# Feed-forward blocks with tokens as the stationary operand and the norm factor in the activation

## The chip, the cores and the metric

The kernel runs on one core of a Trainium2 chip. TensorE (PE) multiplies matrices and transposes, ScalarE (ACT), VectorE (DVE) and GpSimd (POOL) do the work on elements, SyncE (SP) issues the transfers. The metric is the time of one execution on the device in microseconds (us), as the median of several runs.

## The reference

Two stacks of layers over 256 tokens of 1024 channels, all in float32. Around each mixer (recurrent, attention, gated delta rule, short convolution, sparse attention; six in all) stand two feed-forward blocks, twelve in all, and they are what the change is about:

```
def swiglu_2(h, w_gate_up, w_down):              # F = 2816 hidden columns
    g, u = jnp.split(h @ w_gate_up, 2, axis=-1)
    return (jax.nn.silu(g) * u) @ w_down

f = swiglu(rms_norm(h, ffn1_pre_g[layer]), ffn1_w_gate[layer], ffn1_w_up[layer], ffn1_w_down[layer])
h = h + 0.5 * rms_norm(f, ffn1_post_g[layer])    # first stack, 4 blocks: a gain after the block ("post")
h = h + 0.5 * swiglu_2(rmsnorm(h, ffn_norm[layer, 0]), ...)   # second stack, 8 blocks: none
```

`rms_norm(x, g)` is `x * rsqrt(mean(x * x) + eps) * g`. The `shared_kv` of the first stack projects another norm of the same input that a block gets.

## The kernel before

Every product of float32 operands is made of three matmuls, on operands split into a high and a low part (`mm3`, L162 to L164). Weights come through `weights` (L125 to L157): SP loads a unit of 1024 columns into one of five `raw` buffers, ACT writes its high part (L154 with the gain of the norm as a scale, L150 without), DVE the low part (L155, L151). The high and low parts of the gate and up weights live in a pool of six buffers, those of the down weights in another of six.

The 256 tokens are two tiles of 128 (`t` = 0 and 1). `h[t]` is the residual stream in SBUF. `prep` (L194) makes the operand of the next projection: squares on ACT (`rstd`, L189), a small sum on DVE (L190), the power on POOL (L191), then `xn`, the normalized tile, on DVE (L208; L210 where the gain is multiplied in as a row, which holds for the norms before the mixers). Eight transposes of `xn` on PE (L174), a copy on ACT (L175, `xh`) and a subtraction on DVE (L176, `xl`) follow in `flush`.

A block (`ffn`) walks over the hidden columns in 11 groups of 256. Group 0 goes by `rows_group`: tokens are stationary, the weights move 512 columns wide (256 of gate, 256 of up), 24 matmuls for each token tile, and the result has to be transposed. Groups 1 to 10 go by `cols_group`: weights are stationary in pieces of 128 x 128, both token tiles move (256 columns), 96 matmuls for a group; the result is already transposed. `act` (L244 on ACT, L245 and L246 on DVE) makes `hid`, and L292 and L293 split it into `hh` and `hl`. `down_mm` multiplies with the down weights, 12 matmuls of 512 columns for each token tile and group, and runs one group behind. At the end of a block `residual` adds to `h[t]`: L340 without a gain after the block; with one, the squares of the accumulators (L189), a product (L335) and a sum (L336). It then calls `prep`.

The order of the instructions on each engine is fixed when the program is built, by a scheduler that takes the order of the code, the buffers that come free and a priority; the weight conversions are raised by `ahead` places. PSUM has four banks for the accumulators (`acc`), two for the gate and up products (`gu`) and two for transposes (`tr`).

Of the kernel before, what the change touches and what calls it, by code (L numbers as in the profile page):

```python
# [64 lines left out]
class Core:  # L65
# [44 lines left out]
    def rows_to_cols(self, name, *srcs):  # L110
        """srcs: DRAM [n, w] each -> SBUF [w, sum n] with row r in column r."""
# [47 lines left out]
    def mm3(self, out, l, r, start, stop, skip=False):  # L159
        """out += l.T @ r for operands split in (high, low) parts."""  # L160
# [5 lines left out]
    def split_T(self, src, xh, xl):  # L166
        """transpose the 128-column chunks of src [128, *] into xh/xl [128, chunks, 128]"""
# [10 lines left out]
    def by_token(self):  # L178
        """a pair [128, 2, 8, 128] (token tile, chunk, token), high and low"""
# [3 lines left out]
    def rstd(self, parts, scale=1.0):  # L183
        """(mean square of two 512 column parts + eps) ** -0.5, times scale"""
# [6 lines left out]
        nc.gpsimd.tensor_tensor(ss[:, 3:4], ss[:, 2:3], self.mhalf[:, :1], op=OP.pow)  # L191
        return ss[:, 3:4]

    def prep(self, t):  # L194
        """transposed split of h[t], normalized (times row_gain, where there is one), into self.x; the
        transposes are left to flush"""
        nc = self.nc
        self.flush()
        if t == 0:
            self.x = self.by_token()  # L200
        h = self.h[t]
        r = self.rstd([h[:, 0:512], h[:, 512:1024]])
        x, xs = self.x, []
        for n in range(2):
            xn = self.work.tile([128, 512], F32, name="xn", bufs=2)
            s = slice(n * 512, n * 512 + 512)
            if self.row_gain is None:
                nc.vector.tensor_scalar_mul(xn, h[:, s], r)  # L208
            else:
                nc.vector.scalar_tensor_tensor(xn, h[:, s], r, self.row_gain[:, s], op0=OP.mult, op1=OP.mult)  # L210
            xs.append(xn)
# [1211 lines left out]
```

## Time and profile before

| | |
|---|---|
| median of 3 runs | 3331.24 us (3331.01 to 3331.54) |
| the profiled execution: span | 3325.6 us |
| the profiled execution's own time | the span and what lies around it; against the median this is 5.6 us |
| PE, DVE, ACT, POOL busy | 98%, 65%, 54%, 2% |
| chain that ended last | PE 88%, DVE 6%, ACT 3% |
| bytes moved | 543.94 MB, mean 164 GB/s |

A page of the profile describes one execution; its rows name an engine, a line of the kernel, the operands (`out<-in`), and times. Busy time of an engine that nobody waits for costs nothing; what counts is when PE starts its instructions, since PE has work nearly all the time. PEld is the load of the stationary operand, which overlaps with PE.

### The profile page before, as it was taken

The page shows a single profiled execution, that of the slowest core. Times are in us where ns is not written, and L with a number is a line of the kernel's source. Part 1 is how long each engine was busy: PE and PEld are TensorE (multiplying, and loading weights), DVE is VectorE, ACT ScalarE, POOL GpSimd, SP SyncE. Part 2 cuts the span into 40 slices and gives each one's busy share as a digit, 9 for nine tenths or more (in the row PEclk, how much of TensorE's full clock was granted, in tenths as well). Part 3 has the DMA queues.
Part 4 walks back from the last instruction along what each step waited for, and adds up shares of the span by engine and source line. Part 5 has one row for each costly group of instructions (what it writes and reads, how often), then busy time and mean ns, then how long its engine had stood idle before and what let it go on. Part 6 is the DMA issues. An engine that isn't in the chain of part 4 may idle for free.

```text
span 3325.6 us, 57379 instructions
## 1 busy us (share of the span) xinstructions
PE 3266.9 (98%) x22022; PEld 2950.3 (89%) x22022; DVE 2163.9 (65%) x4039; ACT 1781.7 (54%) x3277; POOL 82.1 (2%) x106
## 2 busy tenths in 40 slices
PE   8999999999999999999999999999999999999999
PEld 8988898988798998989999989899767989989898
DVE  7667766664666657776566575665767566577764
ACT  6557655554555544555555455554566555454653
POOL 0000000000000000000000000000100000000000
PEclk9999999998899999999999999999999999999999
DMA  8643665644465663336656466566515656532463
GB/s 265 193 132 120 216 198 169 186 152 129 145 192 160 208 185 109 102 99 206 189 178 198 145 198 195 158 206 188 143 52 164 186 161 205 179 102 86 133 201 109
DMA packets 422043, 543.94 MB, mean 164 GB/s; under 512 B 36232, under 2 KB 369096, under 8 KB 421768
## 3 DMA queue, kind: packets, MB, share of 16 engines
q1 hardware_dynamic: 421768, 540.27, 52.6%
q8 instruction: 173, 2.83, 0.3%
q14 instruction: 102, 0.84, 0.1%
HBM read 539.12 MB, written 1.05 MB: 162 GB/s over the span
## 4 chain that ended last, share of the span: by engine, by line
PE 88%; DVE 6%; ACT 3%; issue 2%; POOL 1%; DMA 1%; POOLq 0%; SPq 0%; ACTq 0%; DVEq 0%
PE ps L164 26%; PE ps L162 26%; PE ps L163 26%; PE ps L174 1%; PE ps L892 1%; PE ps L898 1%; DVE wlo L155 1%; PE ps L1286 1%; DVE wlo L151 1%; POOL ss L191 1%; PE ps L1310 1%; PE ps L725 1%; ACT sq L189 1%; PE ps L554 1%; ACT whi L150 0%
## 5 line engine op out<-in xcount | busy, mean ns | idle before, releaser
L162 PE MATMUL ps<-xh,whi 128*128 128x256 f32 (+1 forms) x4704 | 1335.0, 284 | 6.7 <-ACT v L839 2.7
L164 PE MATMUL ps<-xh,wlo 128*128 128x256 f32 (+1 forms) x4704 | 1333.7, 284 | 0.0
L163 PE MATMUL ps<-xl,whi 128*128 128x256 f32 (+1 forms) x4704 | 1332.8, 283 | 0.0
L155 DVE SCALAR_TENSOR_TENSOR wlo<-raw,gains,whi 128x512 fp32r<-128x512 f32 (+1 forms) x1024 | 717.1, 735 | 470.8 <-ACT whi L154 457.3
L154 ACT ACTIVATE whi<-raw,gains 128x512 fp32r<-128x512 f32 (+1 forms) x1024 | 676.7, 707 | 560.1 <-issue 265.3
L162 PEld LDWEIGHTS ps<-xh,whi 128*128 128x128 f32 (+1 forms) x4704 | 895.6, 190 | 14.1 <-ACT v L839 3.1
L163 PEld LDWEIGHTS ps<-xl,whi 128*128 128x128 f32 (+1 forms) x4704 | 895.9, 190 | 6.0
L164 PEld LDWEIGHTS ps<-xh,wlo 128*128 128x128 f32 (+1 forms) x4704 | 895.3, 190 | 1.2
L151 DVE TENSOR_TENSOR wlo<-raw,whi 128x1024 fp32r<-128x1024 f32 (+4 forms) x473 | 569.6, 1209 | 270.4 <-ACT whi L150 268.0
L150 ACT CAST whi<-raw 128x1024 fp32r<-128x1024 f32 (+4 forms) x473 | 488.9, 1038 | 298.9 <-DMA raw<-in_ffn_w_down 126.0
L162 PE MATMUL ps<-whi,hh 128*128 128x512 f32 x1056 | 412.7, 391 | 0.0
L163 PE MATMUL ps<-wlo,hh 128*128 128x512 f32 x1056 | 412.6, 391 | 0.0
L164 PE MATMUL ps<-whi,hl 128*128 128x512 f32 x1056 | 411.3, 390 | 0.0
L162 PE MATMUL ps<-whi,xh 128*128 128x512 f32 (+3 forms) x624 | 249.2, 400 | 3.0 <-ACT xh L175 3.0
L164 PE MATMUL ps<-whi,xl 128*128 128x512 f32 (+3 forms) x624 | 245.4, 394 | 2.4 <-DVE xl L176 2.4
L163 PE MATMUL ps<-wlo,xh 128*128 128x512 f32 (+3 forms) x624 | 246.0, 394 | 0.0
L164 PEld LDWEIGHTS ps<-whi,hl 128*128 128x128 f32 x1056 | 197.8, 188 | 43.3 <-DVE hl L293 1.8
L162 PEld LDWEIGHTS ps<-whi,hh 128*128 128x128 f32 x1056 | 198.8, 188 | 38.8 <-ACT hh L292 2.0
L163 PEld LDWEIGHTS ps<-wlo,hh 128*128 128x128 f32 x1056 | 198.3, 188 | 37.5
L244 ACT ACTIVATE hid<-ps 128x256 f32<-128x256 f32 x264 | 99.7, 378 | 132.5 <-PE ps L164 132.2
L245 DVE SCALAR_TENSOR_TENSOR hid<-hid,ps 128x256 f32<-128x256 f32 x264 | 110.2, 418 | 74.4 <-ACT hid L244 74.3
L164 PEld LDWEIGHTS ps<-whi,xl 128*128 128x128 f32 (+2 forms) x624 | 116.7, 187 | 28.1 <-DVE xl L176 6.8
(403 smaller groups left out, 2757.2 us busy)
## 6 DMA issues: line engine op xcount, KB each, us to landing
raw<-in_ffn_w_gate_up SPq DMA_DIRECT2D x704, 256.0 KB
raw<-in_ffn_w_down SPq DMA_DIRECT2D x264, 512.0 KB
raw<-in_ffn_w_gate SPq DMA_DIRECT2D x176, 256.0 KB
raw<-in_ffn_w_up SPq DMA_DIRECT2D x176, 256.0 KB
raw<-in_gdn_w_in SPq DMA_DIRECT2D x64, 512.0 KB
raw<-in_sc_w_in SPq DMA_DIRECT2D x24, 512.0 KB
raw<-in_w_kv SPq DMA_DIRECT2D x16, 512.0 KB
raw<-in_gdn_w_out SPq DMA_DIRECT2D x16, 512.0 KB
```

Source lines behind the costliest of these rows:

```text
L150: nc.scalar.copy(hi, raw)
L151: nc.vector.tensor_sub(lo, raw, f32(hi))
L154: nc.scalar.activation(hi[:, i], raw[:, i], AF.Copy, scale=gain[i])
L155: nc.vector.scalar_tensor_tensor(lo[:, i], raw[:, i], gain[i], f32(hi[:, i]), op0=OP.mult, op1=OP.subtract)
L162: mm(out, l[0], r[0], start=start, stop=False, skip_group_check=skip)
L163: mm(out, l[0], r[1], start=False, stop=False, skip_group_check=skip)
L164: mm(out, l[1], r[0], start=False, stop=stop, skip_group_check=skip)
L174: nc.tensor.transpose(p[:, k], src[:, (i + k) * 128:(i + k + 1) * 128], self.ident)
L189: nc.scalar.activation(sq, p, AF.Square, scale=1 / (32.0 * scale), accum_out=ss[:, i:i + 1])
L191: nc.gpsimd.tensor_tensor(ss[:, 3:4], ss[:, 2:3], self.mhalf[:, :1], op=OP.pow)
L244: nc.scalar.activation(hid, p[:, :256], AF.Tanh, scale=0.5)
L245: nc.vector.scalar_tensor_tensor(hid, hid, 1.0, p[:, :256], op0=OP.add, op1=OP.mult)
```

## The change

All groups now run with the tokens stationary. `G(j, t)` is the gate and up product of group `j` and tile `t`, 24 matmuls of 512 columns; `T(j)` transposes the four pieces of `hid`; `D(j, t)` is the down product, 12 matmuls. `prep` no longer normalizes where there is no row gain: `h` itself is transposed, and half of the norm factor goes into a tile `half[t]`, computed after the transposes are issued. `act` takes it: the tanh gets it as scale, and the second product 2 times its square. `shared_kv`, which projects the same operand, multiplies the factor in afterwards.

The order of the code: at the start of a block tile 0 goes two groups ahead before tile 1 is transposed, and at the end tile 0 is finished, and its norm started, before tile 1 has its last gate product. Down weights of a group are shared out over two pools (`wts`, and `fw` with six more buffers).

```diff
-        r = self.rstd([h[:, 0:512], h[:, 512:1024]])
...
+        if self.row_gain is None:
+            self.half[t] = self.work.tile([128, 2], F32, name="half", bufs=6)
+            xs = halves
+        else:
+            r, xs = self.rstd(halves), []
...
         if t == 1:
             self.flush()
+        if self.row_gain is None:
+            f = self.half[t]
+            self.rstd(halves, 0.5, f[:, 0:1])
+            nc.vector.tensor_scalar(f[:, 1:2], f[:, 0:1], f[:, 0:1], 2.0, op0=OP.mult, op1=OP.mult)
...
+        hp = ctx.enter_context(self.tc.tile_pool(name="hid", bufs=2))
+        own = ctx.enter_context(self.tc.tile_pool(name="fw", bufs=6))
...
+            gu[j] = [self.weights([(0, gv[:, 2 * kk:2 * kk + 2, c]), (256, uv[:, 2 * kk:2 * kk + 2, c])],
+                                  [gain[:, 2 * kk + i:2 * kk + i + 1] for i in range(2)],
+                                  pool=self.wts if kk < 2 or j == 0 else own) for kk in range(4)]
...
+            dw[j] = [self.weights([(0, dv[:, 2 * j + k:2 * j + k + 1, :])], None, (1, 1024),
+                                  self.wts if k == 0 and j < 9 else own) for k in range(2)]
...
+        def G(j, t):
+
+            p = self.bank("gu")
+            for k in range(8):
+                wh, wl = gu[j][k // 2]
+                self.mm3(p, (xh[:, t, k], xl[:, t, k]), (wh[:, k % 2], wl[:, k % 2]), k == 0, k == 7)
...
+            nc.scalar.activation(h, p[:, :256], AF.Tanh, scale=half[t][:, 0:1])
+            nc.vector.scalar_tensor_tensor(h, h, 1.0, p[:, :256], op0=OP.add, op1=OP.mult)
+            nc.vector.scalar_tensor_tensor(h, p[:, 256:], half[t][:, 1:2], h, op0=OP.mult, op1=OP.mult)
...
+        def T(j, ts=(0, 1)):
...
+            self.split_T(hid[j][:, 128 * c.start:128 * c.stop], *[a[:, c] for a in hT[j]])
...
+        load_gu(0)
+        G(0, 0)
+        load_gu(1)
+        G(1, 0)
+        self.flush()
+        G(0, 1)
+        G(1, 1)
+        T(0)
+        load_d(0)
+        D(0, 0)
+        T(1)
+        D(0, 1)
+        for j in range(2, 10):
+            load_gu(j)
+            G(j, 0)
+            load_d(j - 1)
+            G(j, 1)
+            D(j - 1, 0)
+            T(j)
+            D(j - 1, 1)
...
+        load_gu(10)
+        G(10, 0)
+        load_d(9)
+        D(9, 0)
+        load_d(10)
+        T(10, (0,))
+        D(10, 0)
+        self.residual(0, acc[0], pg, 0.5)
+        G(10, 1)
+        D(9, 1)
+        self.flush()
+        T(10, (1,))
+        D(10, 1)
+        self.residual(1, acc[1], pg, 0.5)
```

How the instructions stand now is shown at three places. First PE in the middle of a block, where the gate product ends and the down product begins; before (`xh`, `xl` tokens, `whi`, `wlo` weights, `hh`, `hl` hidden values):

```order
L162 MATMUL ps<-xh,whi 128x256
L163 MATMUL ps<-xl,whi 128x256
L164 MATMUL ps<-xh,wlo 128x256
L162 MATMUL ps<-whi,hh 128x512
L163 MATMUL ps<-wlo,hh 128x512
L164 MATMUL ps<-whi,hl 128x512
```

Now, where the second half of the down product of the group before begins:

```order
L162 MATMUL ps<-whi,hh 128x512
L163 MATMUL ps<-wlo,hh 128x512
L164 MATMUL ps<-whi,hl 128x512
L174 MATMUL ps<-ident,hid 128x128 x4
L162 MATMUL ps<-whi,hh 128x512
L163 MATMUL ps<-wlo,hh 128x512
L164 MATMUL ps<-whi,hl 128x512
L162 MATMUL ps<-whi,hh 128x512
```

Four transposes of `hid` stand between the two halves of the down product, twelve matmuls behind the last gate matmul.

Second, DVE over one group in the middle of a block, before (L155 and L151 are weight conversions, L245 and L246 the two products of `act`, L293 the split):

```order
L155 SCALAR_TENSOR_TENSOR wlo<-raw,gains,whi 128x512 x6
L245 SCALAR_TENSOR_TENSOR hid<-hid,ps 128x256
L246 SCALAR_TENSOR_TENSOR hid<-hid,ps 128x256
L155 SCALAR_TENSOR_TENSOR wlo<-raw,gains,whi 128x512
L293 TENSOR_TENSOR hl<-hid,hh 128x256
L245 SCALAR_TENSOR_TENSOR hid<-hid,ps 128x256
L155 SCALAR_TENSOR_TENSOR wlo<-raw,gains,whi 128x512
L246 SCALAR_TENSOR_TENSOR hid<-hid,ps 128x256
L293 TENSOR_TENSOR hl<-hid,hh 128x256
L151 TENSOR_TENSOR wlo<-raw,whi 128x1024 x2
```

Now (L271 and L272 are the two products, L176 the split behind the transposes):

```order
L271 SCALAR_TENSOR_TENSOR hid<-hid,ps 128x256
L272 SCALAR_TENSOR_TENSOR hid<-ps,half,hid 128x256
L155 SCALAR_TENSOR_TENSOR wlo<-raw,gains,whi 128x512 x6
L271 SCALAR_TENSOR_TENSOR hid<-hid,ps 128x256
L155 SCALAR_TENSOR_TENSOR wlo<-raw,gains,whi 128x512
L272 SCALAR_TENSOR_TENSOR hid<-ps,half,hid 128x256
L155 SCALAR_TENSOR_TENSOR wlo<-raw,gains,whi 128x512
L176 TENSOR_TENSOR hl<-ps,hh 128x512
```

The second tile's products still have one weight conversion between them, and the split of both tiles is one instruction.

Third, PE at the end of a block that another block follows, where tile 0 is transposed; before:

```order
L164 MATMUL ps<-whi,hl 128x512
L174 MATMUL ps<-ident,xn 128x128 x8
L162 MATMUL ps<-whi,hh 128x512
L163 MATMUL ps<-wlo,hh 128x512
L164 MATMUL ps<-whi,hl 128x512
```

Now:

```order
L164 MATMUL ps<-whi,hl 128x512
L174 MATMUL ps<-ident,h_90 128x128 x8
L162 MATMUL ps<-whi,xh 128x512
L163 MATMUL ps<-wlo,xh 128x512
L162 MATMUL ps<-whi,xh 128x512
L163 MATMUL ps<-wlo,xh 128x512
L174 MATMUL ps<-ident,hid 128x128 x2
L164 MATMUL ps<-whi,xl 128x512
L162 MATMUL ps<-whi,xh 128x512
L163 MATMUL ps<-wlo,xh 128x512
```

`h_90` is `h[0]`. Before, down matmuls of tile 1 followed the transposes; now the gate matmuls of the next block that read their result do, and tile 1's transposes of `hid` stand among them.

## Rows read from the trace of the kernel before

**Rows 1.** The page: the first section (busy time, share of the span and instructions of each engine) and the fourth (the chain that ended last, by engine and by line).

```profile
PE 3266.9 (98%) x22022; PEld 2950.3 (89%) x22022; DVE 2163.9 (65%) x4039; ACT 1781.7 (54%) x3277; POOL 82.1 (2%) x106
...
PE 88%; DVE 6%; ACT 3%; issue 2%; POOL 1%; DMA 1%; POOLq 0%; SPq 0%; ACTq 0%; DVEq 0%
PE ps L164 26%; PE ps L162 26%; PE ps L163 26%; PE ps L174 1%; PE ps L892 1%; PE ps L898 1%; DVE wlo L155 1%; PE ps L1286 1%; DVE wlo L151 1%; POOL ss L191 1%; PE ps L1310 1%; PE ps L725 1%; ACT sq L189 1%; PE ps L554 1%; ACT whi L150 0%
```

**Rows 2.** The view of instructions grouped by line, engine and operands, different shapes apart: busy us, mean ns of one, and after the second bar the idle time of the engine just before them with what ended it. PE's duration of a matmul overlaps the next one's, so the pace is read from starts (Rows 3).

```profile
L162 PE MATMUL ps<-xh,whi 128*128 128x256 f32 x4512 | 1280.8, 284 | 4.7 <-ACT v L839 2.7 <-ACT whi L150 2.0
...
L155 DVE SCALAR_TENSOR_TENSOR wlo<-raw,gains,whi 128x512 fp32r<-128x512 f32 x984 | 702.0, 747 | 465.6 <-ACT whi L154 452.1 <-DMA raw<-in_ffn_w_gate_up 8.9 <-DMA raw<-in_ffn_w_up 1.5
L154 ACT ACTIVATE whi<-raw,gains 128x512 fp32r<-128x512 f32 x984 | 661.5, 717 | 557.0 <-issue 265.3 <-PE ps L163 219.8 <-DMA raw<-in_ffn_w_gate_up 42.7
...
L162 PE MATMUL ps<-whi,hh 128*128 128x512 f32 x1056 | 412.7, 391 | 0.0
...
L162 PE MATMUL ps<-whi,xh 128*128 128x512 f32 x544 | 220.8, 406 | 2.8 <-ACT xh L175 2.8
...
L164 PE MATMUL ps<-whi,xl 128*128 128x512 f32 x544 | 217.3, 400 | 2.4 <-DVE xl L176 2.4
...
L174 PE MATMUL ps<-ident,xn 128*128 128x128 f32 x288 | 42.2, 284 | 24.2 <-DVE xn L208 15.2 <-DVE xn L210 8.1 <-DVE future L92 0.4
```

**Rows 3.** Windows over one group in the middle of a block: from the start of its first gate matmul (1000.07) to the start of its first down matmul (1011.58) to the start of the next group (1017.05), and the two together. Columns: length, busy time and instructions of each engine, granted TensorE clock as a share of full speed, share of the DMA engines, GB/s.

```profile
1000.07:1011.58 11.51, 11.51 (x98) 11.51 (x96) 5.04 (x8) 4.39 (x7) 0.00 (x0) 1.00 0.58 184
1011.58:1017.05 5.47, 5.47 (x27) 4.51 (x25) 4.93 (x10) 4.21 (x7) 0.00 (x0) 1.00 0.62 193
1000.07:1017.05 16.98, 16.98 (x122) 16.02 (x120) 9.96 (x17) 8.60 (x14) 0.00 (x0) 1.00 0.60 187
```

**Rows 4.** The timeline of PE in a mixer that projects with tokens stationary: matmuls of 512 columns on `xh`, and between two of them four transposes. Columns: start, duration, engine, line, operation, operands.

```profile
1870.20 0.39 PE L162 MATMUL ps<-whi,xh 128*128 128x512 f32 x1
...
1870.88 0.39 PE L162 MATMUL ps<-whi,xh 128*128 128x512 f32 x1
1871.11 0.60 PE L439 MATMUL ps<-ident,y 128*128 128x128 f32 x4
1871.47 0.47 PE L163 MATMUL ps<-wlo,xh 128*128 128x512 f32 x1
1871.78 0.39 PE L164 MATMUL ps<-whi,xl 128*128 128x512 f32 x1
1872.01 0.40 PE L162 MATMUL ps<-whi,xh 128*128 128x512 f32 x1
```

**Rows 5.** The timeline at the end of the gate matmuls of group 0, tile 0, of the first block (the part that already has tokens stationary): the last gate matmul, the activation on ACT, the two products on DVE with a weight conversion between them, and the transposes of `hid`.

```profile
20.66 0.39 PE L164 MATMUL ps<-whi,xl 128*128 128x512 f32 x1
...
21.09 0.39 ACT L244 ACTIVATE hid<-ps 128x256 f32<-128x256 f32 x1 [1.65 <-PE ps L164]
...
21.51 0.42 DVE L245 SCALAR_TENSOR_TENSOR hid<-hid,ps 128x256 f32<-128x256 f32 x1 [0.28 <-ACT hid L244]
...
21.85 0.74 DVE L155 SCALAR_TENSOR_TENSOR wlo<-raw,gain,whi 128x512 fp32r<-128x512 f32 x1
...
22.51 0.41 DVE L246 SCALAR_TENSOR_TENSOR hid<-hid,ps 128x256 f32<-128x256 f32 x1
...
23.16 0.38 PE L174 MATMUL ps<-ident,hid 128*128 128x128 f32 x2
```

**Rows 6.** The timeline at the end of a block without a gain after it (the norm before the next block): `h` is written, PE runs its last down matmul before the wait, the normalized `xn` is made, PE transposes it.

```profile
1666.46 0.69 DVE L340 SCALAR_TENSOR_TENSOR h<-ps,h 128x512 f32<-128x512 f32 x1 [0.23 <-PE ps L164]
...
1668.75 0.39 PE L164 MATMUL ps<-whi,hl 128*128 128x512 f32 x1
1668.82 0.88 DVE L208 TENSOR_SCALAR xn<-h,ss 128x512 f32<-128x512 f32 x2 [0.66 <-POOL ss L191]
...
1669.36 1.11 PE L174 MATMUL ps<-ident,xn 128*128 128x128 f32 x8 [0.22 <-DVE xn L208]
```

**Rows 7.** The same at blocks with a gain after them: squares of the accumulators on ACT (L189), the sum into `h` on DVE (L336) and the transposes; the first two of a block before the recurrent mixer, tile 0 (there the norm that follows has a row gain), the last four of a block before another block, tile 0 and tile 1.

```profile
196.04 0.60 ACT L189 ACTIVATE sq<-ps 128x512 bf16<-128x512 f32 x1
...
202.79 1.32 PE L174 MATMUL ps<-ident,xn 128*128 128x128 f32 x8 [1.35 <-DVE xn L210]
...
523.07 0.60 ACT L189 ACTIVATE sq<-ps 128x512 bf16<-128x512 f32 x1 [0.24 <-PE ps L164]
...
526.05 1.28 DVE L336 TENSOR_TENSOR h<-xn,h 128x512 f32<-128x512 f32 x2
...
528.66 0.58 ACT L189 ACTIVATE sq<-ps 128x512 bf16<-128x512 f32 x1
...
535.15 0.69 DVE L336 TENSOR_TENSOR h<-xn,h 128x512 f32<-128x512 f32 x1
```

**Rows 8.** The timeline of the same block end, tile 1: the eight transposes and the next matmul that reads them.

```profile
538.46 1.06 PE L174 MATMUL ps<-ident,xn 128*128 128x128 f32 x8 [0.86 <-DVE xn L208]
...
539.76 0.50 PE L162 MATMUL ps<-whi,xh 128*128 128x512 f32 x1 [0.24 <-ACT xh L175]
```

**Rows 9.** Windows, columns as in Rows 3: the longest stretch at half the clock, in the attention, and the same length after it.

```profile
802.36:846.73 44.37, 44.37 (x176) 25.12 (x176) 15.96 (x60) 15.94 (x59) 0.00 (x0) 0.50 0.04 13
846.73:891.10 44.37, 40.40 (x211) 29.19 (x211) 29.65 (x55) 28.20 (x59) 2.59 (x4) 1.00 0.41 131
```

More of the change, by code (lines that the diff above doesn't have):

```diff
@@ L236, in ffn @@
         dv = down.rearrange("(k p) n -> p k n", p=128)
[L237 removed]
+        (xh, xl), half = self.x, self.half
         acc = [[None, None], [None, None]]
         ctx = ExitStack()
[L240 to L247 removed]
@@ L250, in down_mm, with D @@
+        def T(j, ts=(0, 1)):
+            if j not in hT:
+                hT[j] = [hp.tile([128, 4, 128], F32R, name=n) for n in ("hh", "hl")]
+            c = slice(2 * ts[0], 2 * ts[-1] + 2)
+            self.split_T(hid[j][:, 128 * c.start:128 * c.stop], *[a[:, c] for a in hT[j]])
+        def D(j, t):
+            hh, hl = [a[:, 2 * t:2 * t + 2] for a in hT[j]]
             for n in range(2):
@@ L253, in down_mm @@
                 s = slice(n * 512, n * 512 + 512)
-                for k in range(len(h)):
-                    self.mm3(acc[t][n], h[k], (w[k][0][:, 0, s], w[k][1][:, 0, s]),
-                             start and k == 0, stop and k == len(h) - 1)
-        def gu_units(j):
-            c = slice(j * 256, j * 256 + 256)
-            return [self.weights([(0, gv[:, 2 * kk:2 * kk + 2, c]), (256, uv[:, 2 * kk:2 * kk + 2, c])],
-                                 [gain[:, 2 * kk + i:2 * kk + i + 1] for i in range(2)]) for kk in range(4)]
@@ L263, in d_units @@
-        def d_units(j):
-            return [self.weights([(0, dv[:, 2 * j + k:2 * j + k + 1, :])], None, (1, 1024), dpool) for k in range(2)]
-        def rows_group(j, t, gu):
-            tok = slice(t * 128, t * 128 + 128)
-            p = self.bank("gu")
-            for k in range(8):
-                wh, wl = gu[k // 2]
-                self.mm3(p, (xh[:, t, k], xl[:, t, k]), (wh[:, k % 2], wl[:, k % 2]), k == 0, k == 7)
-            hid = act(p)
-            hh = dpool.tile([128, 2, 128], F32R, name="hh", bufs=4)
-            hl = dpool.tile([128, 2, 128], F32R, name="hl", bufs=4)
-            self.split_T(hid, hh, hl)
-            return [(hh[:, k], hl[:, k]) for k in range(2)]
@@ L297, in ffn @@
-        pend = None
-        for j in range(10):
-            gu = gu_units(j)
-            if j == 0:
-                hs = [rows_group(j, 0, gu)]
-                self.flush()
-                hs.append(rows_group(j, 1, gu))
-            else:
-                hs = cols_group(j, gu)
-            if pend is not None:
-                dw = d_units(j - 1)
-                for t in range(2):
-                    down_mm(t, pend[t], dw, j == 1, False)
-            pend = hs
+                for k in range(2):
+                    self.mm3(acc[t][n], (hh[:, k], hl[:, k]), (dw[j][k][0][:, 0, s], dw[j][k][1][:, 0, s]),
+                             j == 0 and k == 0, j == 10 and k == 1)
@@ L651, in project_few, with shared_kv @@
             yield t, p
-    def shared_kv(self, C, x, gain, w_kv, w_f, b_f):
+    def shared_kv(self, C, x, half, gain, w_kv, w_f, b_f):
         nc, v = self.nc, self.nc.vector
+        fac = C.tile([128, 2], F32, name="fac")
+        pf = self.bank("tr")
+        for t in range(2):
+            v.tensor_scalar_mul(fac[:, t:t + 1], half[t][:, 0:1], 2.0)
+            nc.tensor.transpose(pf[:, t * 128:t * 128 + 128], fac[:, t:t + 1].to_broadcast([128, 128]), self.ident)
+        frow = C.tile([128, 256], F32, name="frow")
+        v.tensor_copy(frow, pf[:, :256])
         kT = C.tile([128, 8, 256], F32, name="kT")
```

76 lines of the change are left out of this document (23 added, 53 removed).

## The prediction

> **What bounds the kernel now.** I read the page first: PE is busy 98% of the span, and the chain that ended last is 88% PE, spread over the three lines of `mm3` [rows 1]. So the time is, to first order, the sum of the intervals between PE's starts, and a change counts by what it does to them. The grouped view then shows which matmuls these are: 3 x 4512 gate and up matmuls of 256 columns (L162 is a third of them), nearly all in `cols_group`, and 3 x 1056 down matmuls of 512, with almost no idle time before either [rows 2]. The durations in that view (284 and 391 ns) overlap, so the pace comes from windows between starts: one group takes 11.51 us for its 96 matmuls of 256 (0.1199 each) and 5.47 us for 24 of 512 (0.2279 each); in both PE is busy 100% at the full clock of 2.4 GHz, while DVE has 9.96 of 16.98 us, ACT 8.60, and the transfers 0.60 of the DMA engines [rows 3]. Inside a block nothing but PE's own pace counts. The rest of PE's time before work is at block ends: 24.2 us ahead of the transposes of `xn`, 15.2 of them behind L208 and 8.1 behind L210, and 2.8 + 2.4 us ahead of the first matmuls that read `xh` and `xl` [rows 2].
>
> I make the sum against the profiled execution: its span of 3325.6 us and 5.6 us around it are the median of 3331.2.
>
> **Part 1, gate and up product: less.** Groups 1 to 10 of 12 blocks, 120 groups, go from 96 matmuls of 256 to 48 of 512, the same columns in all. At the pace of the down matmuls 48 take 48 x 0.2279 = 10.94 us, 0.57 less than 11.51 [rows 3]; 120 x 0.57 = **-68.4**. That the pace holds with tokens stationary is shown in a mixer: three starts from 1870.20 to 1870.88, 0.227 each [rows 4]. Group 0 has this form already and stays out of the sum.
>
> The Trainium skill ("TensorE: Matmul & The Clock Gate", section "Back-to-back issue gap") gives an isolated matmul of N columns N / 2.4 + 2.5 ns at the full clock, thus a fixed part of only 2.5 ns; halving the count would then save 48 x 2.5 = 0.12 us a group, an estimate of 14.4 us in all, less than the transposes below cost, and the change would lose. The trace disagrees: two of 256 less one of 512 are 2 x 119.9 - 227.9 = 11.9 ns.
>
> **Part 2, transposes: more.** The result has tokens in the partitions, so each of the 120 groups gets four transposes of `hid`. Between matmuls of 512 four transposes add 1872.01 - 1870.88 = 1.13 less 3 x 0.228 = 0.45 us [rows 4]; 120 x 0.45 = **+54.0**. L292 and L293 go, L175 and L176 come, off PE's path: ACT and DVE had 7 to 8 us free in a group [rows 3].
>
> **Part 3, the new wait.** `T(j)` waits for `hid`. In group 0 of the first block the same chain can be timed: the last gate matmul starts at 20.66 (the next would at 20.89); tanh at 21.09; product at 21.51; a conversion; second product at 22.51, done at 22.92; transposes at 23.16 [rows 5]. That is 2.27 us behind 20.89, with one conversion between the products, as the new order of DVE has it. The order puts twelve matmuls in between, 12 x 0.228 = 2.73 us: spare 0.46, wait 0. But if the tanh finds ACT inside a conversion (0.72 us, L154 [rows 2]) it is up to 0.72 later, 2.99 in all, 0.26 too late. Spread evenly over 0 to 0.72 that is 0.26 x 0.26 / 2 / 0.72 = 0.05 a group. Nearest is the row, 0, and I take 0.03: 120 x 0.03 = **+3.6**, ends 0 and +31. What queues behind a late product is the next conversion on DVE; PE behind the transposes has the second half of the down product.
>
> A block's inside is thus -68.4 + 54.0 + 3.6 = -10.8.
>
> **Part 4, block ends.** *Gains.* Without `xn`, tile 0 and 1 of 11 blocks (22 preps) wait for `h` alone. Where no gain stands after the block, `h` was done at 1666.46 + 0.69 = 1667.15 and the transposes came at 1669.36, 0.38 behind the last matmul's slot (1668.75 + 0.23), of which the view counts 0.22 as idle [rows 6]. So the raw path has 2.2 us to spare there. Taking all of L208's 15.2 us [rows 2] and 0.16 more at each of 22: -18.7. Tile 0 ahead of the mixers (row gain, L210) now has `G(10, 1)` and `D(9, 1)` behind its accumulators, some 36 matmuls, 8.2 us, against a chain of 202.79 - 196.04 = 6.75 us [rows 7]: half of L210's 8.1 and 6 x 0.16, -5.0.
>
> *What is late next.* With a gain after the block the raw `h` still needs accumulator squares, power and L335, L336: 523.07 to 526.69 for tile 0, 3.6 us; but 528.66 to 535.84, 7.2 us, for tile 1, where ACT and DVE have the conversion of tile 0 to do [rows 7]. The order puts 15 matmuls (3.4 us) over tile 1 at two block-to-block ends and 20 (4.6) behind the recurrent mixer: late by 2 x 0.2 = 0.4 with the short chain, 2 x 3.8 + 2.6 = 10.2 with the long one; I take +6, nearer the long one since the same engines have the same work. Before the recurrent mixer tile 1's norm has 19 matmuls, 4.3 us, against 6.75: +2.4. After `h_90` the new order has readers of `xh` at once. Such a wait is 539.76 - 538.46 = 1.30 less 8 transposes (2 x 0.45 = 0.9), 0.4, and some 0.3 for `xl`: 0.7 [rows 4, 8]; at 11 ends 7.7, less the 5.2 of this kind that stand there now [rows 2]: +2.5. At the gated-delta mixers only 13 matmuls (3.0 us) separate the tiles: +2. The last `T(10, 1)` has nothing over its conversion, +0.7 by the same wait. Together -18.7 - 5.0 + 6 + 2.4 + 2.5 + 2 + 0.7 = **-10.1**, ends 0 and -23.7.
>
> `shared_kv`'s two transposes and a few products, the power on POOL and the first block's start (where weights, not the norm, come last) I set at nothing: they lie under the gate products; were the cover gone, the power and the product behind it would show as the wait ahead of the transposes does now, 0.2 to 0.4 us [rows 6].
>
> **Sum.** -68.4 + 54.0 + 3.6 - 10.1 = -20.9: 3331.2 - 20.9 = **3310** us.
>
> **Rivals.** *Slower: `hid` comes late at every group.* Conversions are raised in priority; ACT stays in order, so a conversion that waits for its `raw` transfer holds the tanh (L154 already has 42.7 us of idle behind the transfers [rows 2]). With w us of wait a group the total is -24.5 + 120 w; it decides from w = 0.20, and with a conversion in front of the tanh and half of another in front of a product (0.26 + 0.1) w is 0.35: +17.5, 3349. For it: ACT's order has two large casts right ahead of the first tanh. Against: 7 to 8 us free on ACT and DVE in a group [rows 3]. 0.10.
> *No change:* the same with w of 0.14 to 0.25, about 3331. 0.08.
> *Ends give nothing:* the waits for `h` and `xh` take the place of those for `xn`: -10.8, 3320. For it: the 7.2 us chain; against: 2.2 us to spare at the ends without a gain. 0.18.
> *More:* no new waits at the ends (-23.7) or the clock: the stretch at 1.2 GHz in the attention ran 176 PE instructions where the next 44.37 us ran 211 [rows 9]; at that pace it would take 37.0, 7.4 less. The clock fell there with few transfers and long waits, which the change does not touch, so I count it only here: -38 at most, about 3296. 0.10.
> *The 512 pace does not hold* with the new transposes between: at 2 x 0.1199 part 1 yields nothing, 47.5 us more, 3379. Against: [rows 4] show it holds at four transposes. 0.02. The skill's 2.5 ns would make it 3364, by the estimate above.
>
> [...]
>
> **Numbers.** Forecast 0.52, more 0.10, ends give nothing 0.18, no change 0.08, late `hid` 0.10, pace 0.02. A measurement of this kernel tells about 0.2% (6.7 us) from no change: faster is below 3324.6, slower above 3337.9. Faster: 0.52 + 0.10 + 0.11 of the ends' 0.18 (it lies 4 us inside) = 0.73; same 0.07 + 0.08 = 0.15; slower 0.12. The range 3294 to 3334 leaves out the slow cases (0.12) and half of "more" (0.05).
>
> **What would show it.** A window over one group should read 16.98 - 0.57 + 0.45 = 16.86 to 16.89 us, with no idle ahead of L174 `hid` beyond 0.05; over 17.2 the slower rival is right, and the releaser named there tells whether tanh, product or transfer. Idle ahead of the transposes of `h` should be under 8 us where 15.2 stood, and that behind L210 near 4. Idle behind L175 and L176 near 8. Wrong would be: a pace of G above 0.232, or block ends that still sum to 24.

## The result and the profile after

| | median us | runs |
|---|---|---|
| before | 3331.54 | 7, from 3330.5 to 3333.68 |
| changed | 3352.1 | 7, from 3331.4 to 3365.17 |
| ratio | 1.0057 | 95% interval 1.0032 to 1.0082 |
| predicted | 3310 | range 3294 to 3334 |

The change makes the kernel slower by about 0.6%, where a gain of 0.6% was forecast. Executions of the changed kernel also differ by 34 us among themselves, those of the kernel before, in these seven, by 3 (in the later series from 3327 to 3350). They follow the mean granted clock: 3331.4 us at 0.996, 3352.1 at 0.989, 3365.17 at 0.986. The trace shown in this section is the fastest of them (0.996), so totals below are compared at like clocks.

The page: PE is as busy as before [rows 1]; the chain has less PE in it, 82% for 88%, and more transfers, 4% for 1%.

```profile
span 3329.7 us, 46474 instructions
...
PE 3262.4 (98%) x16744; PEld 2688.6 (81%) x16744; DVE 2162.3 (65%) x3902; ACT 1789.4 (54%) x3155; POOL 82.3 (2%) x106
...
PE 82%; DVE 6%; ACT 4%; DMA 4%; issue 2%; POOL 1%; SPq 0%; ACTq 0%; DVEq 0%; POOLq 0%
```

The grouped view, different shapes apart (columns as in [rows 2]):

```profile
L162 PE MATMUL ps<-whi,xh 128*128 128x512 f32 x2464 | 975.5, 396 | 3.4 <-ACT xh L175 2.1 <-DVE hid L272 0.8 <-ACT whi L150 0.5
...
L162 PE MATMUL ps<-whi,hh 128*128 128x512 f32 x1056 | 425.3, 403 | 20.2 <-ACT hh L175 20.2
...
L174 PE MATMUL ps<-ident,hid 128*128 128x128 f32 x528 | 82.2, 274 | 2.8 <-DVE hid L272 2.6
...
L174 PE MATMUL ps<-ident,h 128*128 128x128 f32 x192 | 29.9, 288 | 4.1 <-DVE h L341 2.9 <-DVE h L343 0.6 <-DVE future L92 0.3
L174 PE MATMUL ps<-ident,xn 128*128 128x128 f32 x96 | 14.7, 288 | 8.5 <-DVE xn L212 8.4
```

Two rows answer to the sum: ahead of the transposes of `h` and `xn` stand 4.1 + 8.5 us of idle where 24.2 stood [rows 2], and ahead of those of `hid` 2.8 in all, 2.6 of them one wait in the first block (at 61.75), so the wait of part 3 does not exist in the middle of a block. One row was not in the sum: 20.2 us ahead of the first down matmuls, behind the copy of `hh`.

Windows over one group in the middle of a block (gate product; down product with the transposes in its middle; both):

```profile
1708.93:1720.02 11.09, 11.09 (x50) 9.01 (x48) 6.46 (x9) 5.86 (x9) 0.00 (x0) 1.00 0.41 128
1720.02:1726.00 5.98, 5.98 (x30) 4.89 (x28) 3.80 (x7) 2.91 (x6) 0.00 (x0) 1.00 0.90 287
1708.93:1726.00 17.07, 17.07 (x78) 13.91 (x76) 10.26 (x15) 8.77 (x14) 0.00 (x0) 1.00 0.59 183
```

The 48 gate matmuls take 11.09 us where 10.94 were expected and 11.51 stood [rows 3]; down product and transposes 5.98 (5.47 + 0.45 expected). The group takes 17.07 us: slower than before (16.98), at full clock, with PE never idle. The single starts show how:

```profile
1708.93 0.40 PE L162 MATMUL ps<-whi,xh 128*128 128x512 f32 x1
...
1711.02 0.39 PE L162 MATMUL ps<-whi,xh 128*128 128x512 f32 x1
...
1711.70 0.40 PE L162 MATMUL ps<-whi,xh 128*128 128x512 f32 x1
...
1713.09 0.40 PE L162 MATMUL ps<-whi,xh 128*128 128x512 f32 x1
...
1714.49 0.39 PE L162 MATMUL ps<-whi,xh 128*128 128x512 f32 x1
...
1715.19 0.39 PE L162 MATMUL ps<-whi,xh 128*128 128x512 f32 x1
...
1717.23 0.40 PE L162 MATMUL ps<-whi,xh 128*128 128x512 f32 x1
```

A chunk is the three matmuls on one of the eight pieces of 128 input columns; chunks 0 to 3 have weights in the pool `wts`, 4 to 7 in the pool `fw`. These are the first matmuls of chunks 0, 3, 4 and 6 of tile 0 and of chunks 0, 1 and 4 of tile 1. Chunk 3 takes 0.68 us, 0.227 for each matmul; the six matmuls behind it 1.39, 0.232 each; the next six 1.40, 0.233. The pace changes where the weights change from `wts` to `fw`. On the way back it changes late: in tile 1 chunk 0 still takes 0.70 and chunks 1 to 3 then 0.227 for each matmul; in tile 0 chunks 0 to 2, behind the down product, take 0.232.

At the start of a block the timeline shows the new wait:

```profile
1969.82 0.82 PE L174 MATMUL ps<-ident,hid 128*128 128x128 f32 x6
...
1970.63 1.34 ACT L154 ACTIVATE whi<-raw,gains 128x512 fp32r<-128x512 f32 x2 [0.41 <-DMA raw<-in_ffn_w_gate_up]
...
1971.87 0.45 ACT L270 ACTIVATE hid<-ps,half 128x256 f32<-128x256 f32 x1
...
1973.13 0.72 ACT L154 ACTIVATE whi<-raw,gains 128x512 fp32r<-128x512 f32 x1 [0.81 <-DMA raw<-in_ffn_w_gate_up]
...
1973.76 0.56 ACT L175 CAST hh<-ps 128x512 fp32r<-128x512 f32 x1
...
1974.38 0.50 PE L162 MATMUL ps<-whi,hh 128*128 128x512 f32 x1 [2.59 <-ACT hh L175]
```

PE transposes `hid` of group 0 at 1969.82. In the middle group above the copy (L175) comes 0.7 us behind the transposes (1722.80 and 1723.49); but here, on ACT, which works in order, weight conversions (L154), which have to wait for their transfers, and the tanh of group 1 stand ahead of it. It comes at 1973.76, and PE, which has only five matmuls left to do, waits 2.59 us.

### The profile page after: what moved, and what is told of

It is laid out like the page before. It is cut to its first block, busy times and chain, and to the rows that moved or that the text cites. A ratio compares the mean times of both kernels' runs of the same rounds, so it can differ in the third digit from the quotient of the medians.

```text
span 3329.7 us, 46474 instructions
## 1 busy us (share of the span) xinstructions
PE 3262.4 (98%) x16744; PEld 2688.6 (81%) x16744; DVE 2162.3 (65%) x3902; ACT 1789.4 (54%) x3155; POOL 82.3 (2%) x106
## 4 chain that ended last, share of the span: by engine, by line
PE 82%; DVE 6%; ACT 4%; DMA 4%; issue 2%; POOL 1%; SPq 0%; ACTq 0%; DVEq 0%; POOLq 0%
PE ps L162 24%; PE ps L164 24%; PE ps L163 24%; PE ps L174 2%; DVE wlo L155 2%; DMA raw<-in_ffn_w_gate_up 2%; ACT whi L154 1%; PE ps L904 1%; PE ps L910 1%; DMA raw<-in_ffn_w_up 1%; DVE wlo L151 1%; PE ps L1298 1%; PE ps L1322 1%; PE ps L559 1%; PE ps L737 1%
## 5 line engine op out<-in xcount | busy, mean ns | idle before, releaser
L162 PE MATMUL ps<-whi,xh 128*128 128x512 f32 (+2 forms) x2544 | 1004.2, 395 | 3.5 <-ACT xh L175 2.1
L164 PE MATMUL ps<-whi,xl 128*128 128x512 f32 (+2 forms) x2544 | 999.9, 393 | 0.0
L163 PE MATMUL ps<-wlo,xh 128*128 128x512 f32 (+2 forms) x2544 | 999.0, 393 | 0.0
L155 DVE SCALAR_TENSOR_TENSOR wlo<-raw,gains,whi 128x512 fp32r<-128x512 f32 (+1 forms) x1024 | 709.7, 735 | 108.4 <-ACT whi L154 104.5
L154 ACT ACTIVATE whi<-raw,gains 128x512 fp32r<-128x512 f32 (+1 forms) x1024 | 670.0, 706 | 143.7 <-PE ps L164 69.4
L151 DVE TENSOR_TENSOR wlo<-raw,whi 128x1024 fp32r<-128x1024 f32 (+4 forms) x473 | 561.9, 1209 | 270.3 <-ACT whi L150 266.8
L162 PEld LDWEIGHTS ps<-whi,xh 128*128 128x128 f32 (+2 forms) x2544 | 477.2, 188 | 109.3 <-ACT xh L175 5.8
L163 PEld LDWEIGHTS ps<-wlo,xh 128*128 128x128 f32 (+2 forms) x2544 | 477.1, 188 | 103.1 <-issue 0.7
L164 PEld LDWEIGHTS ps<-whi,xl 128*128 128x128 f32 (+2 forms) x2544 | 476.5, 187 | 102.9 <-issue 0.5
L162 PE MATMUL ps<-whi,hh 128*128 128x512 f32 x1056 | 425.3, 403 | 20.2 <-ACT hh L175 20.2
L270 ACT ACTIVATE hid<-ps,half 128x256 f32<-128x256 f32 x264 | 124.6, 472 | 483.5 <-PE ps L164 478.9
L271 DVE SCALAR_TENSOR_TENSOR hid<-hid,ps 128x256 f32<-128x256 f32 x264 | 110.3, 418 | 350.5 <-ACT hid L270 350.3
L162 PE MATMUL ps<-xh,whi 128*128 128x256 f32 (+2 forms) x864 | 247.9, 287 | 6.7 <-ACT v L851 2.7
L164 PE MATMUL ps<-xh,wlo 128*128 128x256 f32 (+2 forms) x864 | 248.6, 288 | 0.0
L163 PE MATMUL ps<-xl,whi 128*128 128x256 f32 (+2 forms) x864 | 246.5, 285 | 0.0
L175 ACT CAST hh<-ps 128x512 fp32r<-128x512 f32 x144 | 79.1, 549 | 192.6 <-PE ps L174 192.6
```

The source lines that it names most:

```text
L151: nc.vector.tensor_sub(lo, raw, f32(hi))
L154: nc.scalar.activation(hi[:, i], raw[:, i], AF.Copy, scale=gain[i])
L155: nc.vector.scalar_tensor_tensor(lo[:, i], raw[:, i], gain[i], f32(hi[:, i]), op0=OP.mult, op1=OP.subtract)
L162: mm(out, l[0], r[0], start=start, stop=False, skip_group_check=skip)
L163: mm(out, l[0], r[1], start=False, stop=False, skip_group_check=skip)
L164: mm(out, l[1], r[0], start=False, stop=stop, skip_group_check=skip)
```

## The experiments

The same program again, for another execution's trace.

> The changed kernel unaltered, to see more executions of it. Its one trace so far has a mean granted clock of 0.996 and 3331 us, while other executions had down to 0.986 and 3365 us. Theory C (the waits at block starts trip the clock): the executions spread by more than 15 us again, the slower the lower the clock, about 3 us for each 0.001; if the trace kept is one below 0.994, its stretches at half the clock begin within some 6 us of a wait of 1.5 us or more at a block start. Rival C' (the denser stream of 512 columns itself lowers the clock): such stretches begin in the middle of blocks, with no wait before them.

Measured: 3356.19 us (3343.19 to 3363.05), ratio 1.0062 (1.0039 to 1.0085). The trace kept has a clock of 0.988 and a span of 3356.3. Windows over the same piece of the attention, of the first trace and of this one, and of the stretch at half the clock in the second:

```profile
737.46:872.49 135.03, 133.62 (x891) 108.00 (x889) 84.65 (x210) 80.67 (x188) 3.01 (x4) 1.00 0.44 136
```

```profile
739.19:893.23 154.04, 152.63 (x890) 117.61 (x889) 84.88 (x210) 81.00 (x189) 3.01 (x4) 0.86 0.39 119
811.10:855.47 44.37, 44.37 (x177) 25.11 (x175) 16.07 (x61) 16.07 (x59) 0.00 (x0) 0.50 0.05 13
```

The same work (891 and 890 records of PE) takes 135.03 us or 154.04: the stretch of 44.37 us at 1.2 GHz costs 19 us. PE is busy all through it, before the fall as well, so no wait that the profile shows explains it. The trace of before has the same stretch [rows 9], and the clocks of its executions (all at 0.991 or less) suggest that it nearly always has. Falls of 3.41 us behind a wait at a block start are there too (two in this trace, behind waits of 2.30 and 2.19 us; eight others of 1.39 to 3.66 us have none), but by the two levels of the clock each costs at most 3.41 / 2 = 1.7 us. Theory C accounts at most for these short ones; the large part of the spread is the attention's, which neither theory named. The wait ahead of the first down matmuls is here:

```profile
L162 PE MATMUL ps<-whi,hh 128*128 128x512 f32 x1056 | 425.8, 403 | 22.9 <-ACT hh L175 22.9
```

Next, the pools sorted by kind:

```diff
-                                  pool=self.wts if kk < 2 or j == 0 else own) for kk in range(4)]
+                                  pool=self.wts if kk < 2 or j != 1 else own) for kk in range(4)]
...
-                                  self.wts if k == 0 and j < 9 else own) for k in range(2)]
+                                  own) for k in range(2)]
```

> Gate and up weights of all groups but group 1 in the pool wts, all down weights in the pool fw; the order of the code is as changed. In the changed kernel a middle group takes 17.07 us where the sum gave 16.88: matmuls of 512 run at 0.227 us with weights of wts and tokens, and at 0.233 with weights of fw and tokens, and at 0.2315 in the down product, whose two weights come from the two pools. Theory P (the pace depends on which buffers the two operands of neighbouring matmuls lie in): a middle group falls to 16.75 to 16.90, the whole by 15 to 30 us at equal clock. Rival P' (the pace is set by the traffic of ACT, DVE and transfers, or by the transposes): 17.07 and the same time within 5 us. The waits at block starts stay at about 20 us in all, and the spread stays.

Measured: 3308.53 us (3305.38 to 3328.74), ratio 0.9936 (0.9917 to 0.9956). In seven of ten executions the clock was 0.993 or more; the three others lay at 3323 to 3329. At like clocks (0.987, 0.989, 0.993, 0.996) it is 26 to 34 us under the changed kernel. A middle group takes 16.83 us, its gate product 10.89:

```profile
1748.80:1765.63 16.83, 16.83 (x77) 13.91 (x76) 10.00 (x16) 8.56 (x14) 0.00 (x0) 1.00 0.61 188
1748.80:1759.69 10.89, 10.89 (x50) 9.01 (x48) 6.48 (x10) 5.21 (x8) 0.00 (x0) 1.00 0.43 122
```

Theory P holds. The waits at the start fell too, to 14.0 us; that this comes from another order of the conversions was not shown.

Which property of a pool it is, 128 unused bytes tell:

```diff
+        ctx.enter_context(self.tc.tile_pool(name="pad", bufs=1)).tile([128, 32], F32, name="pad")
         hp = ctx.enter_context(self.tc.tile_pool(name="hid", bufs=2))
```

> The changed kernel with 128 unused bytes of each partition ahead of the pools hid and fw, so that every buffer of a block stands at the same offset within 512 bytes as the buffers of wts and of xh and xl; nothing else is altered. If P holds because of the offset of the two operands within some small block of memory, a middle group falls from 17.07 to 16.75 to 16.90 us as when pools are sorted by kind. If P holds because the two pools lie far apart, or because of something else that goes with the pool, it stays at 17.07, within 0.03.

Measured: 3339.36 us (3313.64 to 3351.55), ratio 0.9998 (0.9971 to 1.0025); a middle group takes 16.79 to 16.81 us (gate product 10.88, down product with transposes 5.92):

```profile
1754.15:1770.94 16.79, 16.79 (x77) 13.91 (x76) 10.21 (x15) 8.79 (x14) 0.00 (x0) 1.00 0.57 183
1754.15:1765.03 10.88, 10.88 (x49) 9.01 (x48) 6.38 (x9) 5.84 (x9) 0.00 (x0) 1.00 0.40 125
```

The median hides it, since these ten executions had lower clocks (0.980 to 0.994): at 0.988 and 0.992 they are 29 to 34 us under the changed kernel, which is about 120 x 0.26 = 31. The offset decides, not the distance. The late changes of pace at the start of the gate product are gone with it: there every chunk takes 0.68 us. In the built program `wts` begins at byte 51072 of a partition and `xh` at 100224, both 128 past a multiple of 256; `fw` at 163072 and `hh` at 154880, both at a multiple of 256. In the kernel before `fw`'s predecessor and `hh` (159808, 151616) stood at 64 past one, together.

The sweep, one number of bytes for each block (in the changed kernel a middle group takes 17.07 us in all twelve):

```diff
+        n = (0, 32, 64, 96, 128, 160, 192, 224, 256, 320, 384, 448)[self.blocks]
...
+            ctx.enter_context(self.tc.tile_pool(name="pad", bufs=1)).tile([128, n // 4], F32, name="pad")
```

> The changed kernel with another number of unused bytes ahead of hid and fw in each of the 12 blocks: 0, 32, 64, 96, 128, 160, 192, 224, 256, 320, 384, 448. Only the time of a middle group in each block is read, 17.07 us at 0 and 16.81 at 128 as known. Theory O: it depends on the offset alone. If the block of memory is 512 bytes, only 128 gives 16.81; if it is 256, 384 does too; if nearness is enough, 96 and 160 lie between 16.81 and 17.07. If the theory is wrong, the groups of different blocks don't follow the bytes.

Measured in one execution (3353.72 us), the median time from group to group, in us:

| bytes | 0 | 32 | 64 | 96 | 128 | 160 | 192 | 224 | 256 | 320 | 384 | 448 |
|---|---|---|---|---|---|---|---|---|---|---|---|---|
| group | 17.07 | 17.12 | 17.11 | 17.13 | 16.81 | 17.10 | 17.06 | 17.13 | 17.07 | 17.11 | 16.81 | 17.06 |

The transposes of two neighbouring groups, with 0, 128 and 384 bytes:

```profile
111.95 0.60 PE L175 MATMUL ps<-ident,hid 128*128 128x128 f32 x4
129.02 0.60 PE L175 MATMUL ps<-ident,hid 128*128 128x128 f32 x4
...
1160.49 0.60 PE L175 MATMUL ps<-ident,hid 128*128 128x128 f32 x4
1177.28 0.60 PE L175 MATMUL ps<-ident,hid 128*128 128x128 f32 x4
...
2846.43 0.60 PE L175 MATMUL ps<-ident,hid 128*128 128x128 f32 x4
2863.24 0.60 PE L175 MATMUL ps<-ident,hid 128*128 128x128 f32 x4
```

Only 128 and 384 are fast; 256 gives what 0 gives. So a group goes at full pace where the two operands stand at the same place within 256 bytes, and nearness is no help. Why the offset counts, no run here shows.

The same in the kernel before, where nothing else is altered:

```diff
             if pend is not None:
+                if j == 1:
+                    dpool.tile([128, 32], F32, name="pad", bufs=1)
                 dw = d_units(j - 1)
```

> The kernel before with 128 unused bytes between the buffers of hh and hl and those of the down weights, which stood at one offset within 512 bytes; nothing else is altered. Theory O (a matmul of 512 goes at 0.227 us where its stationary and its moving operand stand at the same offset within some small block of memory, and at about 0.233 where they don't): 24 down matmuls take 5.54 to 5.62 us instead of 5.47, 120 groups make the kernel 8 to 18 us slower, 3340 to 3352. Rival: the pace belongs to the new order or to its transposes, and here nothing changes: 5.47, within 3 us.

Measured: 3343.85 us (3339.22 to 3361.45), ratio 1.0045 (1.0027 to 1.0063). The 24 down matmuls of a group, which took 5.47 [rows 3]:

```profile
1001.75:1007.33 5.58, 5.58 (x27) 4.54 (x26) 4.58 (x10) 4.21 (x7) 0.00 (x0) 1.00 0.53 170
```

120 x 0.11 = 13 us expected from that, 12 measured (against 3332.06 for the kernel before in that series). Theory O holds without the change.

Now the start of a block, one group ahead instead of two, all else as changed:

```diff
-        load_gu(1)
-        G(1, 0)
         self.flush()
         G(0, 1)
-        G(1, 1)
+        load_gu(1)
+        G(1, 0)
         T(0)
         load_d(0)
+        G(1, 1)
         D(0, 0)
```

> Only the start of a block is undone: tile 0 goes one group ahead instead of two, and 24 gate matmuls stand between each transposes of hid and the down product that reads them. Theory S (the 20 us of idle ahead of the first down matmuls are the copy of hh, late on ACT behind weight conversions that wait for their transfers): that idle falls below 5 us in all and the total by 12 to 20 us at equal clock. With theory C the clock then stays at 0.990 or more and the executions lie within 6 us of each other: 3305 to 3318 us. Rival S': the wait moves, to the transposes of tile 1 of h or to the weights of group 1, and the total stays within 6 us of the changed kernel. Rival C': the spread of 15 us and more stays.

Measured: 3331.6 us (3315.8 to 3348.61), ratio 0.9988 (0.9965 to 1.0012). The grouped view:

```profile
L162 PE MATMUL ps<-whi,hh 128*128 128x512 f32 x1056 | 423.9, 401 | 0.5 <-ACT hh L175 0.5
...
L174 PE MATMUL ps<-ident,hid 128*128 128x128 f32 x528 | 84.1, 274 | 7.6 <-DVE hid L272 7.3
```

The idle behind `hh` is gone, 5 us of it came back ahead of `hid`; the median is 25 us under that of the changed kernel run again, and at like clocks (0.987, 0.989, 0.996) it is 16 to 22 lower. Theory S holds. The spread stays (33 us), against theory C: with no wait of that kind the attention and the sparse attention still ran at half the clock in the trace kept (41 and 55 us).

Both repairs:

> Both repairs together: the start of a block goes one group ahead, and 128 unused bytes bring the buffers of a block to the same offset within 512 bytes as those of wts and the tokens. Alone the first took the idle ahead of the first down matmuls from 20 us to 0.5, the second a middle group from 17.07 to 16.81 us. If they add (theories P by offset, and S), a middle group takes 16.81 us, that idle stays under 2 us, and the total lies 22 to 28 us below the 3331.6 of the start alone: 3302 to 3312 us, about 0.8% under the kernel before, with the fastest executions (those in which the attention keeps the full clock) at 3285 to 3295. If the shift only helped by chance (it also moves transfers in time), it is within 8 us of 3331.

Measured: 3311.18 us (3298.85 to 3324.07), ratio 0.9935 (0.9916 to 0.9953). They add: with the run below it is 41 to 52 us under the changed kernel at like clocks (0.987, 0.989, 0.996), where the start alone had 16 to 22 and the shift alone 29 to 34; the median is 20 us under that of the start alone, 22 to 28 were expected. Part of the wait comes back ahead of `hid`:

```profile
L174 PE MATMUL ps<-ident,hid 128*128 128x128 f32 x528 | 84.5, 275 | 11.1 <-DVE hid L273 10.7
```

Run again:

> The kernel with both repairs (start one group ahead, 128 bytes) again, as the base of the next two. So far six executions lay from 3299 to 3324 us, the dearest with long stretches at half the clock in the attention and in the sparse attention. Two theories of that spread: the two long stretches come and go by themselves from execution to execution (then the trace kept here has one, both or none of them, each worth 14 to 20 us, and the blocks take the same time, 190 us from one to the next, in any case), or they follow from the blocks (then the blocks differ too).

Measured: 3312.02 us (3286.48 to 3323.06), ratio 0.9927 (0.9894 to 0.9959). The trace has both long stretches, 44.37 us each; the blocks with no fall in them take 188 to 190 us in both traces of this kernel. So the stretches do not follow from the blocks; what sets them off stays open.

With both repairs, and the norm made ahead of the transposes again:

```diff
-            self.half[t] = self.work.tile([128, 2], F32, name="half", bufs=6)
-            xs = halves
+            self.half[t] = self.const_half
...
+                nc.vector.tensor_scalar_mul(xn, halves[n], r)
```

> The kernel with both repairs, but prep normalizes again: xn is made ahead of the transposes at every norm, and the activation gets the constant 0.5 (the offsets of the buffers are kept equal within 512 bytes). It undoes the part of the change that takes the norm factor into the activation. Theory E (at block ends the raw h saves what stood ahead of the transposes of xn): 12 to 22 us more than the kernel with both repairs at equal clock, with 12 to 18 us of idle ahead of the transposes behind L208's successor. Rival E' (the new order of the end alone hides the norm, since tile 0 is finished 36 matmuls earlier): under 6 us more.

Measured: 3334.53 us (3316.07 to 3338.34), ratio 0.9997 (0.9981 to 1.0013): the medians are 22 to 23 us apart from those with raw `h`, and at like clocks (0.985, 0.987) it is 18 to 24 more. The rows of both repairs, and of this kernel:

```profile
L162 PE MATMUL ps<-whi,xh 128*128 128x512 f32 x2464 | 971.6, 394 | 2.1 <-ACT xh L175 2.1
...
L174 PE MATMUL ps<-ident,h 128*128 128x128 f32 x192 | 29.8, 288 | 4.1 <-DVE h L342 3.0 <-DVE h L344 0.5 <-DVE future L92 0.3
...
L174 PE MATMUL ps<-ident,xn 128*128 128x128 f32 x96 | 14.5, 282 | 8.8 <-DVE xn L212 8.7
```

```profile
L164 PE MATMUL ps<-whi,xh 128*128 128x512 f32 x2464 | 974.2, 395 | 4.5 <-ACT xh L177 4.0 <-DVE wlo L157 0.5
L166 PE MATMUL ps<-whi,xl 128*128 128x512 f32 x2464 | 967.5, 393 | 2.3 <-DVE xl L178 2.3
...
L176 PE MATMUL ps<-ident,xn 128*128 128x128 f32 x288 | 42.0, 287 | 29.1 <-DVE xn L213 19.5 <-DVE xn L215 8.7 <-DVE future L92 0.4
```

Theory E holds: ahead of the transposes stand 29.1 us of idle for 4.1 + 8.8 with raw `h`, and ahead of the readers of `xh` and `xl` 6.8 for 2.1, 21 us in all.

With both repairs, the transposes of group 1 later:

```diff
         D(0, 0)
-        T(1)
         D(0, 1)
...
             G(j, 0)
+            if j == 2:
+                T(1)
             load_d(j - 1)
```

> Both repairs, and at the start of a block the transposes of group 1 come behind tile 0 of group 2 (24 matmuls later). There PE still waits 11 us in all for the second product, which is late behind conversions whose transfers are late. If the wait is only a matter of cover, it falls under 4 us and the total by 5 to 9 us at equal clock. If the transfers are late by more than the cover, the wait comes back ahead of the matmuls of group 2 for its weights, and the total stays within 3 us.

Measured: 3293.06 us (3273.02 to 3294.0), ratio 0.9859 (0.982 to 0.9899). The wait was a matter of cover:

```profile
L174 PE MATMUL ps<-ident,hid 128*128 128x128 f32 x528 | 81.6, 273 | 0.2
```

The 11.1 us with both repairs are gone, and the total is 13 to 18 us lower at the same clock (0.989, 0.996), more than the 5 to 9 expected.

With both repairs, the end of a block in pairs:

```diff
         G(10, 0)
         load_d(9)
-        D(9, 0)
+        G(10, 1)
         load_d(10)
-        T(10, (0,))
+        D(9, 0)
+        T(10)
         D(10, 0)
         self.residual(0, acc[0], pg, 0.5)
-        G(10, 1)
         D(9, 1)
         self.flush()
-        T(10, (1,))
         D(10, 1)
```

> Both repairs, and the end of a block as in its middle: both tiles' gate products of group 10 first, then the down products tile by tile, as in the kernel before. It undoes the early finish of tile 0. Theory: with 24 matmuls fewer behind tile 0's accumulators its norm (6.75 us in the chain before) is late at the mixers by about 1.3 us at each of six, and where a gain follows the block the raw h by less than 1 us; 5 to 12 us more than the kernel with both repairs at equal clock. Rival: the raw h needs so little time that the order of the end is free: within 3 us, with the idle ahead of the transposes of xn up by no more than 3 us.

Measured: 3295.84 us (3281.76 to 3303.59), ratio 0.9882 (0.9849 to 0.9915); at a clock of 0.990 3300 against 3304 to 3306, at 0.991 3292 against 3299, at 0.996 3282 against 3286. The rival holds and more: finishing tile 0 early gains nothing, its order costs 4 to 7 us.

All the useful parts together:

> The parts that the runs spoke for, together: gate products with tokens stationary, raw h, buffers at equal offsets, a start one group ahead with the transposes of group 1 behind tile 0 of group 2, and the end in pairs. If the last two add, it lies 3 to 7 us under the 3293 us of the kernel with the late transposes at equal clock, 3286 to 3290 with the attention at half the clock as there, and about 20 us less in executions in which the attention keeps the full clock. If the early finish of tile 0 was of use together with the late transposes, it is above 3293.

Measured: 3285.82 us (3266.54 to 3289.04), ratio 0.9843 (0.9814 to 0.9873), the best of all, 1.6% under the kernel before. Four of the six executions, with clocks of 0.989 to 0.991, lie from 3285.6 to 3289.0, as expected if the last two parts add. The page of its fastest kind of execution (clock 0.996, the attention at full clock):

```profile
span 3267.6 us, 46444 instructions
...
PE 3224.9 (99%) x16744; PEld 2690.0 (82%) x16744; DVE 2154.8 (66%) x3890; ACT 1790.7 (55%) x3141; POOL 80.3 (2%) x106
```

## Why the prediction was wrong

It took the whole for a sum of PE's intervals, and that view was right: each term below is one. Two terms failed: the pace of the gate product, and a wait at the start of a block that was put at nothing.

**Part 1, the pace of the gate product.** "That the pace holds with tokens stationary is shown in a mixer" is the step that failed. It does not hold where the weights lie in the pool `fw`, at another offset within 256 bytes than the tokens. The term came to 120 x (11.51 - 11.09) = -50 instead of -68.4, and the down product lost 0.06 a group by the same cause, 7 us. Where offsets agree, the step is right and the gain even a little larger: 10.88 us, not 10.94. The mixer's rows [rows 4] could not show it, since there weights and tokens stand at one offset; nor could [rows 3], where `hh` and the down weights do. The sign of being wrong that the prediction named, a pace above 0.232, did not show it either: the gate product as a whole went at 11.09 / 48 = 0.231. The rival on the pace had 0.02 and put the blame on the transposes; it feared 0.012 us more for each matmul, and 0.003 came.

**The start of a block.** It was in no term: "the first block's start" was "set at nothing", the other eleven not priced. But `T(0)` now has five matmuls behind it before the down product reads its result, and ACT's order puts conversions that wait for transfers ahead of the copy: 20 to 23 us. The slower rival had this mechanism (a conversion that waits for its transfer, in order on ACT) at every group instead; in the middle of a block there is no wait.

**Part 2** is right: 5.92 - 5.47 = 0.45 a group with equal offsets, as worked out. **Part 3** is right in that no wait stands in the middle of a block; that 2.8 us meet the 3.6 is luck, since 2.6 of them are one wait in the first block.

**Part 4** is about right in its sum and not in its items. Idle ahead of `h` and `xn` fell by 24.2 - 12.6 = 11.6, and the raw `h` itself is worth some 21 us with the new order and both repairs, where 18.7 was the forecast. But half of L210's wait was to go by the early finish of tile 0, and 8.4 us are left of 8.1: tile 0's share did go, from 4.7 to 0.5 us over the six mixers, but tile 1's rose from 3.4 to 7.9; 3.8 of that stand ahead of the recurrent mixer (at 218.35), where none stood and 2.4 were predicted. The end in pairs is better. Of the dearest new wait forecast, +6 for `h` behind a gain, 2.9 came in all (L341), and the +2.5 for the readers of `xh` and `xl` came out as -2 (3.4 for 5.2). The 3.6 us taken there for tile 0 end with the first half of `h` and the 7.2 for tile 1 with the second; by the same row tile 0 takes 526.05 + 1.28 - 523.07 = 4.3 to its second half [rows 7].

**The clock** was priced by the number of PE's instructions, 7.4 us for the stretch in the attention. By the same work at either level it is 19 (the windows above). That the clock fell there with long waits was a wrong reading: PE is busy in 44.37 of the 44.37 us [rows 9]. The statement that the change does not touch it was half right: the stretch is the attention's own, but with the change it comes in some executions and not in others.

Against the trace with that stretch the changed kernel has 3356.3 - 3325.6 = 30.7 us more. The terms: groups 120 x (17.07 - 16.98) = +11; block starts +23; idle at the ends 12.7 in that trace for 24.2, -11.5; waits for `xh` and `xl` 3.4 for 5.2, -2. That leaves some 10; 10 us more at half the clock in the sparse attention than in the trace before are a part of it, and the rest is not taken apart further. The medians are 21 to 23 us apart, and for that the terms suffice.

With both repairs the kernel lies 21 us under the one before, the -20.9 of the sum, but that is in part luck: the groups give 120 x -0.17 = -20 where parts 1 to 3 had -10.8, the ends -11 and -3 where part 4 had -10.1, and the 11 us ahead of `hid` stood in no term.

The Trainium skill ("TensorE: Matmul & The Clock Gate", section "Back-to-back issue gap") has a fixed part of 2.5 ns for an isolated matmul. In these streams, at equal offsets, the traces show 2 x 119.9 - 227 = 13 ns, so the prediction's estimate of a loss by that figure, though of the right sign, rests on the wrong cause.

## What to carry to other kernels

Where a stream of matmuls changes pace with nothing else on the chip in its way, look where its operands stand: in this kernel the pace held where the offsets of the stationary and of the moving buffers within 256 bytes agreed, and a pool that is added or a small tile can shift them. In a software pipeline the dear places are its two ends: count there what stands between a producer and its reader on every in-order engine, conversions and their transfers too. And when executions differ by more than the effect, take several traces and compare equal pieces of work before explaining the total.

## What was not expected of the hardware

Matmuls of 512 columns of float32 data start 0.227 us apart where both operands stand at one offset modulo 256 bytes, and 0.231 to 0.233 apart where the offsets differ, in steps of the new kernel and of the old one alike; in the sweep a difference of 32 bytes cost as much as one of 128. The slower pace goes on for 3 to 9 matmuls behind such a stretch, though their own offsets agree.

A stretch of 44.37 us in the attention (40.96 in three traces) runs at 1.2 GHz in some executions of a program and at 2.4 in others, with PE busy all the time in both, and costs 19 us; a second one, in the sparse attention, goes from 14 to 55 us at half the clock. In 14 traces of all these kernels the first was absent three times. What sets either off stays open.

The tanh before and after the change:

```profile
L244 ACT ACTIVATE hid<-ps 128x256 f32<-128x256 f32 x264 | 99.7, 378 | 132.5 <-PE ps L164 132.2
```

```profile
L270 ACT ACTIVATE hid<-ps,half 128x256 f32<-128x256 f32 x264 | 124.6, 472 | 483.5 <-PE ps L164 478.9
```

With the norm factor as a scale in memory it took 472 ns where 378 stood with a constant, 94 more. The Trainium skill ("ScalarE: Activation LUTs", section "What ACT_TABLE_LOAD costs") gives about 93 ns for each such operand; the trace agrees.
